# Interleaving the products of consecutive row pairs in the down projection

## The chip, the cores and the metric

The kernel runs on one core of a Trainium2 chip. The metric is device time in microseconds (us), the median of several executions. The engines are named as in the profile: PE (TensorE matmul), PEld (its weight loads), DVE (VectorE), ACT (ScalarE), POOL (GpSimd) and SP (SyncE, which here only issues DMAs).

## What is computed

One layer of a streaming encoder: adaptive RMSNorm, an input projection that feeds gated DeltaNet and windowed attention, an output projection, and a ConvFFN. The change lies in the last step, the down projection `y = mid @ w_down` with its gated residual:

```
h2 = rms_norm(x, norm2_w) * (1 + scale2) + shift2
u = h2 @ w_up
u_c = causal_dwconv(u_ext, ffn_conv_w) + ffn_conv_b
gt, up = jnp.split(u_c, 2, axis=-1)
x = x + gate2 * ((jax.nn.silu(gt) * up) @ w_down)
```

There are 640 tokens, 2048 model channels and 5632 hidden channels, all float32.

## The kernel before

A float32 product is made of three matmuls in a faster type: each operand is split into a high part (a cast on ACT) and a low part (source minus high part, on DVE), and high·high, high·low and low·high are summed in PSUM.

**The stage.** The down projection runs in `down` (lines 1984 to 2062). The first 4 of the 44 blocks of hidden channels are multiplied plainly. The other 40 form 5 groups of 8 blocks, and each group takes 8 **jobs**, one for each pair (f, f+8) of output row blocks. So there are 40 jobs (`njobs`, line 2027). A job is a 2x2 block product by Winograd's scheme in **seven products**, numbered 1 to 7. A product is 12 matmuls of 128 columns of weights against 320 tokens: 4 pieces of the contraction by 3 split parts.

**The order of a job.** `WINO` (line 18) gives 1, 5, 6, 2, 7, 3, 4. A job takes two PSUM tiles of two banks each (line 2038): `mmd` (called a) and `mm2` (called b; the profile calls it `mm`). Product 1 opens a bank of a, products 2 and 5 open the two banks of b. `ONTO` (line 19) lets the others accumulate on what is there: 6, 7 and 4 onto the bank of 1, 3 onto the bank of 5. After each product DVE adds what the bank then holds to an output tile `y` (line 2046), so a later product may write into the bank only after that addition has read it. The two tiles have two buffers each, so the next job starts on fresh ones.

**Weights.** SP loads a tile `raw` of weights; two serve a job. ACT casts it (`whi`), DVE subtracts (`wlo`); products 5, 6, 7 and 3 need a sum of two weight blocks first (`wsum`), which DVE makes for 5, 6 and 3 and POOL for 7 (`DPOOL`, line 36). `next_unit` (line 396) keeps this three products ahead of the matmuls: the cast and the subtraction for the unit three later stand ahead of a product's matmuls in the program, and the addition `y` stands behind them. Each engine's queue is worked in order.

**The fill.** While a group's jobs run, `fill` (line 1936) prepares the operands of the next group. It loads blocks `mq` of the hidden activations, forms sums `t`, and splits each into `dop` (two operands, hi and lo). Its steps are slipped in between matmuls as a planner's clock allows.

**Output.** `y` is kept in DRAM (`yd`) between groups: a job's two tiles are loaded (`load`, behind the fourth product of the job before) and stored at the end (`late`, issued by `tail`). In the last group there is no fill; instead a residual tile `xo` is loaded from `xd` behind product 5, `resid` adds the gated result into it (`xo` and `rst` on DVE, a small `xo` on POOL) once a quarter of the output is complete, and each quarter is stored to `out_yT`. All these DMAs stand in the one queue of SP, in program order.

Of the kernel before, what the change touches and what calls it, by code (L numbers as in the profile page):

```python
# [6 lines left out]
F32 = mybir.dt.float32  # L7
# [3 lines left out]
ALU = mybir.AluOpType  # L11
# [3 lines left out]
P = 128  # L15
GRP = 4
ORDER = (2, 4, 5, 1, 6, 7, 3)
WINO = (1, 5, 6, 2, 7, 3, 4)
ONTO = {6: 1, 7: 1, 4: 1, 3: 5}
NF = 8  # L20
NP = 5
# [14 lines left out]
DPOOL = {7: 1}  # L36
# [191 lines left out]
class Kern:  # L228
# [81 lines left out]
    def build_stream(self):  # L310
        d = self.d
        self.units, self.upos, self.spos, self.apos, self.rpos = [], 0, 0, 0, 0
        self.rorder, self.rleft, self.rtile, self.utile, self.ltile = [], {}, {}, {}, {}
        for g in range(4):
            for i in range(3):
                self.add_unit(0, (("e", i, g), d["win"][i, :, g // 2, (g % 2) * 512:(g % 2 + 1) * 512]))
        for i in range(3, 44):
            self.add_block(("in", i), d["win"][i])
        for f in range(KC):
            self.add_block(("o", f), d["wo"][f])  # L320
        for f in range(KC - NF, KC):
# [12 lines left out]
        for i in range(NFF):  # L334
            quarters("u", i, ORDER[4:] if i < NP else ORDER, i < NP)
        n = 0
        for split, m in DGRP:
            for u in range(0 if split else 4 * m):
                self.add_unit(u % 2, (("d", n + u // 2), d["wdn"][n + u // 2]))
            for f in range(8 if split else 0):  # L340
                a = [[(("d", n + 2 * f + j), d["wdn"][n + 2 * f + j], r) for r in range(2)] for j in range(2)]
                t = {k: (("s", n + 2 * f, k), None, 0) for k in (5, 6)}
                for p, src, op in ((1, (a[0][0],), None), (5, (a[1][0], a[1][1]), ALU.add),
                                   (6, (t[5], a[0][0]), ALU.subtract), (2, (a[0][1],), None),
                                   (7, (a[0][0], a[1][0]), ALU.subtract), (3, (a[0][1], t[6]), ALU.subtract),
                                   (4, (a[1][1],), None)):
                    self.add_unit(tuple(x[2] for x in src), *(x[:2] for x in src), op=op, pool=DPOOL.get(p),
                                  keep=t[p][0] if p in t else None)
            n += 2 * m

    def issue_raw(self):
        while self.rpos < len(self.rorder) and not self.rleft.get(self.rraw.peek(), 0):
# [1583 lines left out]
    def fill(self, dp, c0, key):  # L1936
# [24 lines left out]

        for d in range(2):
            b = {}
            for n, (r, s) in enumerate(((0, 0), (0, 1), (1, 1), (1, 0))):
                b[r, s] = ox.tile([P, 2, HALF], F32, tag=f"ex{4 + n}", name="mq")
                k = c0 + 4 * r + 2 * d
                nc.sync.dma_start(out=b[r, s], in_=self.mdt[k:k + 2, :, s * HALF:(s + 1) * HALF].rearrange(
                    "k p c -> p k c"))
            t1, t2, t3, t4 = (dp.tile([P, 2, HALF], F32, tag="stg", name=f"t{n + 1}", bufs=4) for n in range(4))
            yield from put(1, b[0, 0])  # L1970
            yield (b[0, 1],)
            v.tensor_tensor(out=t1, in0=b[0, 1], in1=b[0, 0], op=ALU.subtract)
            yield from put(5, t1)
            yield (b[1, 1],)
            v.tensor_tensor(out=t3, in0=b[1, 1], in1=b[0, 1], op=ALU.subtract)
            v.tensor_tensor(out=t2, in0=t3, in1=b[0, 0], op=ALU.add)
            yield from put(6, t2)
            yield from put(2, b[1, 0])
            yield from put(7, t3)
            yield from put(3, b[1, 1])  # L1980
            v.tensor_tensor(out=t4, in0=b[1, 0], in1=t2, op=ALU.subtract)
            yield from put(4, t4)

    def down(self, dp):
# [11 lines left out]
        def tail():  # L1996
            while late:
                late.pop(0)()
# [16 lines left out]
            return [self.yd[n % 8 + 8 * i].rearrange("p (s c) -> p s c", s=2) for i in range(2)]  # L2015

        def load(n):
            ts = [ox.tile([P, 2, HALF], F32, tag=f"ex{2 * (n % 2) + i}", name=f"y{i}") for i in range(2)]
            for t, d in zip(ts, rows(n)):
                nc.sync.dma_start(out=t, in_=d)  # L2020
            return ts
# [5 lines left out]
        njobs = 8 * (len(DGRP) - 1)  # L2027
        ys = {0: load(0)}
        dest = {1: (0, 0), 5: (1, 1), 6: (0, 1), 2: (0, 0), 7: (1, 1), 3: (0, 1), 4: (1, 0)}
        for n in range(njobs):  # L2030
            f, g = n % 8, n // 8
            last = g == len(DGRP) - 2
            if f == 0 and not last:
                lane.add(self.fill(dp, DGRP[0][1] + 8 * (g + 1), g + 2))
            while g + 1 not in self.dops:
                self.pump()
            self.ops = self.dops[g + 1]
            a, b = self.main_ps2(0)[0], self.main_ps2(1)[0]
            banks = {1: a[:, 0, 0:HALF], 2: b[:, 0, 0:HALF], 5: b[:, 1, 0:HALF]}
            for q, pr in enumerate(WINO):  # L2040
                ps = self.product(pr, None, 1, banks[ONTO.get(pr, pr)], pr not in ONTO)
                if f == 7:
                    self.done.add(("p", g + 1, pr))
                r, h = dest[pr]
                y = ys[n][r][:, h]
                v.tensor_tensor(out=y, in0=y, in1=ps, op=ALU.add)
                if q == 1:
                    tail()
                if q == 3 and n + 1 < njobs:
                    ys[n + 1] = load(n + 1)  # L2050
                if q == 1 and last:
                    x = [dp.tile([P, 2, HALF], F32, tag="stg", name="xo", bufs=4) for _ in range(2)]
                    for i in range(2):
                        nc.sync.dma_start(out=x[i], in_=self.xd[f + 8 * i].rearrange("p (s c) -> p s c", s=2))
                if last and q > 2:
                    k = f + 8 * r
                    self.resid(dp, "rst", x[r][:, h], y, 5, k, h)
                    late.append(lambda x=x[r][:, h], k=k, h=h: nc.sync.dma_start(
                        out=self.o["yT"][:, k, h * HALF:(h + 1) * HALF], in_=x))
            if not last:  # L2060
                late.append(lambda n=n, ts=ys.pop(n): store(n, ts))
        tail()

# [135 lines left out]
```

## Time and profile before

| | us |
|---|---|
| median of 3 runs (3095.6 to 3096.77) | 3095.79 |
| the profiled execution | 3097.97 |
| its span, first to last instruction | 3096.2 |
| plain blocks end, 40 jobs begin (from the span's start) | 2547.4 |
| last group begins | 2973.9 |
| last instruction of DVE ends, about | 3091.7 |

The times below are microseconds from the start of the span. The 40 jobs are the last 544 us of it. Job 0 begins at 2547.4, job 11 at 2693.3, job 15 at 2748.0, jobs 20 to 22 run from 2816.3 to 2853.3, and the last group is jobs 32 to 39. In the timeline a matmul's duration (0.31) is longer than the distance to the next one, since matmuls overlap; the bracket at the end of a row is the time for which the engine sat idle before it, and what released it.

### The profile page before, as it was taken

The numbers are of one execution on the slowest core, as the hardware profiler recorded it, in microseconds if no ns is written. First come the engines' busy times: TensorE is split into PE (matmuls) and PEld (weight loads), VectorE is DVE, ScalarE is ACT, GpSimd is POOL, SyncE is SP. The second block draws the span as 40 slices with busy tenths as digits, with TensorE's granted clock in tenths as the row PEclk, the third lists the DMA queues.
The fourth block names the chain that finished last, engine by engine and source line by source line (L and its number), as shares of the span: only waits on it lengthen the run. The fifth ranks groups of instructions, "written<-read, shape, count | busy, mean of one in ns | idle before, by whom it ended". The sixth has DMA issues, their size and how long they took to land.

```text
span 3096.2 us, 52887 instructions
## 1 busy us (share of the span) xinstructions
PE 2943.2 (95%) x19649; PEld 2765.0 (89%) x19649; DVE 2291.0 (74%) x4419; ACT 1225.0 (40%) x2255; POOL 843.9 (27%) x1283
## 2 busy tenths in 40 slices
PE   5999999999999999987899999999999999999998
PEld 2688889998989988976899999999999999999987
DVE  4333436778886523599798899999899969989887
ACT  2332334333433312453344444444444454444432
POOL 2110012323333321266433333333333311111012
PEclk8999999999999999998999999999999999999999
DMA  8755532222223588646533333333332366655654
GB/s 339 283 179 177 189 119 84 77 79 78 87 76 120 192 292 299 215 137 197 177 97 103 107 97 98 103 102 97 107 105 96 96 226 204 216 193 199 206 201 162
DMA packets 219234, 480.73 MB, mean 155 GB/s; under 512 B 52082, under 2 KB 87184, under 8 KB 218960
## 3 DMA queue, kind: packets, MB, share of 16 engines
q1 hardware_dynamic: 185056, 429.99, 41.6%
q0 software_dynamic: 11152, 36.11, 3.5%
q10 hardware_dynamic: 22768, 11.25, 1.4%
q8 instruction: 155, 2.54, 0.3%
q14 instruction: 103, 0.84, 0.1%
HBM read 407.92 MB, written 71.18 MB: 155 GB/s over the span
## 4 chain that ended last, share of the span: by engine, by line
PE 41%; DVE 6%; DMA 3%; issue 2%; SPq 1%; POOL 0%; ACT 0%; DVEq 0%; POOLq 0%; ACTq 0%
PE mmd L90 21%; PE mm L90 19%; DVE wlo L90 2%; DVE y L90 1%; DVE dop L90 1%; DMA xo<-xd 1%; DVE wsum L90 1%; SPq L90 1%; DMA fext<-pd 1%; DMA y<-yd 1%; DVE t L90 1%; DVE ftm L90 0%; DMA e<-pd 0%; DVE xo L90 0%; DMA yd<-y 0%
## 5 line engine op out<-in xcount | busy, mean ns | idle before, releaser
L90 DVE TENSOR_TENSOR wlo<-raw,whi 128x512 fp32r<-128x512 f32 x584 | 441.4, 761 | 306.6 <-ACT whi L90 278.5
L90 ACT CAST whi<-raw 128x512 fp32r<-128x512 f32 x584 | 358.2, 619 | 553.6 <-PE mm L90 333.5
L90 ACT CAST whi<-wsum 128x512 fp32r<-128x512 f32 x600 | 367.2, 619 | 403.8 <-PE mmd L90 141.8
L90 DVE TENSOR_TENSOR wlo<-wsum,whi 128x512 fp32r<-128x512 f32 x600 | 422.7, 705 | 19.9 <-ACT whi L90 14.1
L90 DVE TENSOR_TENSOR wsum<-raw 128x512 f32<-128x512 f32 x455 | 357.1, 785 | 79.5 <-DMA raw<-in_wup 75.3
L90 PE MATMUL mm<-mh,wlo 128*128 128x320 f32 x1280 | 374.2, 313 | 10.1 <-DVE wlo L90 10.0
L90 PE MATMUL mm<-mh,whi 128*128 128x320 f32 x1280 | 373.8, 312 | 9.3 <-DVE qsq L90 8.1
L90 PE MATMUL mm<-ml,whi 128*128 128x320 f32 x1280 | 372.9, 312 | 0.6 <-DVE ml L90 0.6
L90 PE MATMUL mm<-hh,wlo 128*128 128x320 f32 x1376 | 331.4, 322 | 5.5 <-DVE wlo L90 5.5
L90 PE MATMUL mm<-hh,whi 128*128 128x320 f32 x1376 | 328.6, 320 | 4.5 <-ACT hh L90 3.2
L90 PE MATMUL mm<-hl,whi 128*128 128x320 f32 x1376 | 327.6, 320 | 0.3 <-DVE hl L90 0.3
L90 PE MATMUL mmd<-dop,whi 128*128 128x320 f32 x1280 | 287.2, 312 | 31.2 <-DVE y L90 29.8
L90 PEld LDWEIGHTS mm<-mh,wlo 128*128 128x128 f32 x1280 | 235.2, 189 | 24.0 <-DVE wlo L90 12.2
L90 PEld LDWEIGHTS mm<-mh,whi 128*128 128x128 f32 x1280 | 235.4, 189 | 20.5 <-issue 7.1
L90 PEld LDWEIGHTS mm<-hh,whi 128*128 128x128 f32 x1376 | 230.7, 191 | 21.9 <-issue 13.7
L90 PEld LDWEIGHTS mm<-hh,wlo 128*128 128x128 f32 x1376 | 231.5, 191 | 19.4 <-issue 11.6
L90 PEld LDWEIGHTS mmd<-dop,whi 128*128 128x128 f32 x1280 | 213.8, 189 | 39.1 <-ACT whi L90 25.7
L90 PEld LDWEIGHTS mm<-hl,whi 128*128 128x128 f32 x1376 | 230.9, 191 | 19.4 <-issue 16.5
L90 PEld LDWEIGHTS mm<-ml,whi 128*128 128x128 f32 x1280 | 235.2, 189 | 7.8 <-issue 6.7
L90 PE MATMUL mmd<-mh,wlo 128*128 128x320 f32 x768 | 233.2, 310 | 6.5 <-DVE wlo L90 6.5
L90 PE MATMUL mmd<-mh,whi 128*128 128x320 f32 x768 | 233.0, 310 | 1.1 <-ACT qacc L90 1.1
L90 PE MATMUL mmd<-ml,whi 128*128 128x320 f32 x768 | 232.7, 310 | 0.5 <-DVE ml L90 0.4
(418 smaller groups left out, 6397.3 us busy)
## 6 DMA issues: line engine op xcount, KB each, us to landing
raw<-in_wup SPq DMA_DIRECT2D x206, 512.0 KB, 3.7
araw<-in_adaw SPq DMA_DIRECT2D x256, 256.0 KB, 5.2
raw<-in_wdn SPq DMA_DIRECT2D x88, 512.0 KB, 4.1
raw<-in_win SPq DMA_DIRECT2D x82, 512.0 KB, 3.6
araw<-in_adaw SPq DMA_DIRECT2D x64, 512.0 KB, 6.3
yd<-y SPq DMA_DIRECT2D x80, 320.0 KB, 4.9
y<-yd SPq DMA_DIRECT2D x80, 320.0 KB, 3.8
raw<-in_wo SPq DMA_DIRECT2D x48, 512.0 KB, 5.3
```

The source lines that it names most:

```text
L90: return f(*args, **kw)
```

## The change

The seven products keep their formulas and their banks. Their order changes, and products of two consecutive jobs are interleaved. `PLACE` gives each product a place on a common scale, on which a job begins every 7 places. From the third job on, seven products in a row are 2 of job n, 7 of job n-1, 1 of n, 5 of n, 4 of n-1, 6 of n, 3 of n. The operands are filled in the order 2, 1, 5, 6, 3 and 7, 4 likewise. The output tiles `y` get three buffers for two, and two of the four `mq` tiles move to another pool. The load of the next job's `y` moves behind product 6 (it stood behind product 2, the fourth), that of `xo` behind product 2, the first, and stores are issued behind products 2 and 5.

```
-WINO = (1, 5, 6, 2, 7, 3, 4)
+WINO = (2, 1, 5, 6, 3, 7, 4)
+PLACE = {2: 0, 1: 2, 5: 3, 6: 5, 3: 6, 7: 8, 4: 11}
...
+    def djobs(self):
+
+        todo = sorted((7 * n + PLACE[p], n, p) for n in range(8 * (len(DGRP) - 1)) for p in PLACE)
+        return [x[1:] for x in todo]
...
-            for n, (r, s) in enumerate(((0, 0), (0, 1), (1, 1), (1, 0))):
-                b[r, s] = ox.tile([P, 2, HALF], F32, tag=f"ex{4 + n}", name="mq")
+            for n, (r, s) in enumerate(((1, 0), (0, 0), (0, 1), (1, 1))):
+                b[r, s] = (ox if n < 2 else dp).tile([P, 2, HALF], F32, tag=f"ex{6 + n}", name="mq")
...
+            yield from put(2, b[1, 0])
             yield from put(1, b[0, 0])
...
+            yield (t3,)
             v.tensor_tensor(out=t2, in0=t3, in1=b[0, 0], op=ALU.add)
             yield from put(6, t2)
-            yield from put(2, b[1, 0])
+            yield from put(3, b[1, 1])
             yield from put(7, t3)
-            yield from put(3, b[1, 1])
...
-            ts = [ox.tile([P, 2, HALF], F32, tag=f"ex{2 * (n % 2) + i}", name=f"y{i}") for i in range(2)]
+            ts = [ox.tile([P, 2, HALF], F32, tag=f"ex{2 * (n % 3) + i}", name=f"y{i}") for i in range(2)]
...
-        for n in range(njobs):
+        part, x = {}, {}
+        for n, pr in self.djobs():
...
+            ps = self.product(pr, None, 1, part[n][ONTO.get(pr, pr)], pr not in ONTO)
...
+            if pr in (2, 5):
+                tail()
+            if pr == 6 and n + 1 < njobs:
+                ys[n + 1] = load(n + 1)
+            if pr == 2 and last:
+                x[n] = [dp.tile([P, 2, HALF], F32, tag="stg", name="xo", bufs=4) for _ in range(2)]
+                for i in range(2):
+                    nc.sync.dma_start(out=x[n][i], in_=self.xd[f + 8 * i].rearrange("p (s c) -> p s c", s=2))
```

What this does to the queues, at two places. First DVE in a job without fill. `y0` and `y1` are the two output tiles of a job; the number behind `mmd` or `mm2` tells the jobs apart. Before, the additions are of products 6, 2, 7, 3 and 4 of one job:

```order
L90 TENSOR_TENSOR y0_31091<-y0_31091,mmd_31150 128x320
L90 TENSOR_TENSOR wsum_31209<-raw_31019 128x512
L90 TENSOR_TENSOR wlo_31212<-raw_30872,whi_31211 128x512
L90 TENSOR_TENSOR y0_31091<-y0_31091,mm2_31151 128x320
L90 TENSOR_TENSOR wsum_31234<-wsum_31209,raw_30935 128x512
L90 TENSOR_TENSOR wlo_31237<-raw_30935,whi_31236 128x512
L90 TENSOR_TENSOR y1_31092<-y1_31092,mmd_31150 128x320
L90 TENSOR_TENSOR wlo_31254<-wsum_31209,whi_31253 128x512
L90 TENSOR_TENSOR y0_31091<-y0_31091,mm2_31151 128x320
L90 TENSOR_TENSOR wlo_31273<-wsum_31234,whi_31272 128x512
L90 TENSOR_TENSOR y1_31092<-y1_31092,mmd_31150 128x320
```

In the changed program they are 7 of job n-1, 1 and 5 of job n, 4 of job n-1, 6 and 3 of job n:

```order
L91 TENSOR_TENSOR y1_30948<-y1_30948,mmd_30969 128x320
L91 TENSOR_TENSOR wlo_31153<-wsum_31110,whi_31152 128x512
L91 TENSOR_TENSOR y0_31087<-y0_31087,mmd_31108 128x320
L91 TENSOR_TENSOR wlo_31174<-wsum_31131,whi_31173 128x512
L91 TENSOR_TENSOR y1_31088<-y1_31088,mm2_31109 128x320
L91 TENSOR_TENSOR wlo_31191<-raw_30998,whi_31190 128x512
L91 TENSOR_TENSOR y1_30948<-y1_30948,mmd_30969 128x320
L91 TENSOR_TENSOR wsum_31207<-raw_31032 128x512
L91 TENSOR_TENSOR wlo_31210<-wsum_31169,whi_31209 128x512
L91 TENSOR_TENSOR y0_31087<-y0_31087,mmd_31108 128x320
L91 TENSOR_TENSOR wlo_31231<-raw_30998,whi_31230 128x512
L91 TENSOR_TENSOR y0_31087<-y0_31087,mm2_31109 128x320
```

One tile of PSUM was read at every second addition; now `mmd_30969`, `mmd_31108` and `mm2_31109` are each read at every third. The operations are the same ones.

Second, SP in the last group. Before:

```order
L90 DMA raw<-in_wdn 128x1024
L90 DMA out_yT<-xo 128x320 x4
L90 DMA xo<-xd 128x640 x2
L90 DMA raw<-in_wdn 128x1024
L90 DMA y_33222<-yd 128x640
L90 DMA y_33223<-yd 128x640
```

In the changed program:

```order
L91 DMA y_33385<-yd 128x640
L91 DMA y_33386<-yd 128x640
L91 DMA out_yT<-xo 128x320 x2
L91 DMA xo<-xd 128x640 x2
L91 DMA raw<-in_wdn 128x1024 x2
L91 DMA out_yT<-xo 128x320 x2
```

The load of `xo` stood behind a load of weights and four stores of outputs; now it stands behind the loads of `y` and two stores (of product 4 of the job before last and of product 3 of the last), and the two loads of weights follow it.

## Rows read from the trace of the kernel before

**Rows 1.** The page: busy time, share of the span and instructions of PE.
```profile
PE 2943.2 (95%) x19649; PEld 2765.0 (89%) x19649; DVE 2291.0 (74%) x4419; ACT 1225.0 (40%) x2255; POOL 843.9 (27%) x1283
```

**Rows 2.** Busy time of each engine in stretches of the jobs; granted clock, DMA.
```profile
core 0: us, PE busy (x) PEld busy (x) DVE busy (x) ACT busy (x) POOL busy (x), PEclk, DMA share, GB/s
2547.40:2973.90 426.50, 403.03 (x2690) 395.75 (x2689) 379.26 (x652) 177.29 (x303) 44.32 (x32) 1.00 0.61 204
2816.30:2853.30 37.00, 37.00 (x255) 37.00 (x254) 30.54 (x52) 13.07 (x21) 3.91 (x3) 1.00 0.59 196
...
2706.00:2711.00 5.00, 3.09 (x14) 3.12 (x15) 3.42 (x7) 0.76 (x2) 0.00 (x0) 0.76 0.35 133
...
2973.90:3091.70 117.80, 102.05 (x676) 98.75 (x674) 97.79 (x197) 32.92 (x53) 29.16 (x38) 1.00 0.53 182
2986.80:3063.20 76.40, 63.93 (x422) 61.59 (x421) 62.57 (x126) 21.73 (x35) 20.14 (x25) 1.00 0.56 194
```

**Rows 3.** Waits of PE, jobs 0 to 31: us in total, times, longest.
```profile
PE mmd L90 <- DVE y L90: 15.3, 18, 2.0
PE mm L90 <- DVE y L90: 5.7, 6, 1.2
PE mmd L90 <- ACT whi L90: 1.2, 2, 0.7
```

**Rows 4.** Waits of PE in the last group.
```profile
PE mmd L90 <- DVE y L90: 14.5, 13, 1.7
```

**Rows 5.** Waits of DVE in the last group.
```profile
DVE xo L90 <- DMA xo<-xd: 10.8, 6, 2.3
```

**Rows 6.** Timeline in job 15: start, us, engine, operation, idle before it.
```profile
2752.16 0.48 DVE L90 TENSOR_TENSOR y<-y,mm 128x320 f32<-128x320 f32 x1
...
2757.48 0.81 DVE L90 TENSOR_TENSOR t<-mq,t 128x640 f32<-128x640 f32 x1
2758.21 0.48 DVE L90 TENSOR_TENSOR y<-y,mm 128x320 f32<-128x320 f32 x1
...
2758.84 0.53 PE L90 MATMUL mm<-dop,whi 128*128 128x320 f32 x2 [1.15 <-DVE y L90]
```

**Rows 7.** Timeline of DVE in job 20, without fill.
```profile
2823.47 0.68 DVE L90 TENSOR_TENSOR wlo<-raw,whi 128x512 fp32r<-128x512 f32 x1
2824.07 0.47 DVE L90 TENSOR_TENSOR y<-y,mm 128x320 f32<-128x320 f32 x1
2824.46 0.68 DVE L90 TENSOR_TENSOR wsum<-wsum,raw 128x512 f32<-128x512 f32 x1
```

**Rows 8.** Groups of DVE instructions in the jobs: busy, mean ns | idle before.
```profile
L90 DVE TENSOR_TENSOR wsum<-raw 128x512 f32<-128x512 f32 x39 | 41.2, 1055 | 0.0
L90 DVE TENSOR_TENSOR wsum<-raw,wsum 128x512 f32<-128x512 f32 x39 | 26.6, 683 | 0.0
```

**Rows 9.** Groups of POOL instructions in the jobs.
```profile
L90 POOL TENSOR_TENSOR wsum<-raw 128x512 f32<-128x512 f32 x39 | 53.4, 1369 | 401.3 <-DVE wlo L90 389.9 <-DVE dop L90 11.4
```

**Rows 10.** Chain of waits in job 35: start, us, what.
```profile
3021.77 0.33 SPq L90
...
3024.11 4.47 DMA xo<-xd
```

**Rows 11.** Timeline of DVE in job 35.
```profile
3026.04 0.49 DVE L90 TENSOR_TENSOR y<-y,mm 128x320 f32<-128x320 f32 x1
3028.70 0.48 DVE L90 SCALAR_TENSOR_TENSOR xo<-y,mod,xo 128x256 f32<-128x256 f32 x1 [2.17 <-DMA xo<-xd]
```

**Rows 12.** Timeline of SP ahead of job 11.
```profile
2689.05 1.98 SPq L90 DMA_DIRECT2D mq<-md  x4
2691.12 0.92 SPq L90 DMA_DIRECT2D y<-yd  x2
```

**Rows 13.** Timeline of DVE in job 11, the first addition.
```profile
2697.22 0.49 DVE L90 TENSOR_TENSOR y<-y,mmd 128x320 f32<-128x320 f32 x1 [1.81 <-PE mm L90]
```

**Rows 14.** Timeline of DVE in job 0, the first addition.
```profile
2552.23 0.49 DVE L90 TENSOR_TENSOR y<-y,mmd 128x320 f32<-128x320 f32 x1 [2.41 <-DMA y<-yd]
```

More of the change, by code (lines that the diff above doesn't have):

```diff
@@ L335, in build_stream @@
             quarters("u", i, ORDER[4:] if i < NP else ORDER, i < NP)
[L336 to L349, printed above, removed]
+        n = DGRP[0][1]
+        for u in range(16 * n // 4):
+            self.add_unit(u % 2, (("d", u // 2), d["wdn"][u // 2]))
+        for job, p in self.djobs():
+            f = 2 * n + 2 * job
+            a = [[(("d", f + j), d["wdn"][f + j], r) for r in range(2)] for j in range(2)]
+            t = {k: (("s", f, k), None, 0) for k in (5, 6)}
+            src, op = {1: ((a[0][0],), None), 5: ((a[1][0], a[1][1]), ALU.add), 6: ((t.get(5), a[0][0]), ALU.subtract),
+                       2: ((a[0][1],), None), 7: ((a[0][0], a[1][0]), ALU.subtract),
+                       3: ((a[0][1], t.get(6)), ALU.subtract), 4: ((a[1][1],), None)}[p]
+            self.add_unit(tuple(x[2] for x in src), *(x[:2] for x in src), op=op, pool=DPOOL.get(p),
+                          keep=t[p][0] if p in t else None)
+    def djobs(self):
+        todo = sorted((7 * n + PLACE[p], n, p) for n in range(8 * (len(DGRP) - 1)) for p in PLACE)
+        return [x[1:] for x in todo]
     def issue_raw(self):
@@ L2029, in down @@
         dest = {1: (0, 0), 5: (1, 1), 6: (0, 1), 2: (0, 0), 7: (1, 1), 3: (0, 1), 4: (1, 0)}
-        for n in range(njobs):
+        part, x = {}, {}
+        for n, pr in self.djobs():
             f, g = n % 8, n // 8
             last = g == len(DGRP) - 2
[L2033 to L2036, printed above, removed]
-            self.ops = self.dops[g + 1]
[L2038 to L2060, printed above, removed]
@@ new lines, in down @@
+            if pr == WINO[0]:
+                if f == 0 and not last:
+                    lane.add(self.fill(dp, DGRP[0][1] + 8 * (g + 1), g + 2))
+                while g + 1 not in self.dops:
+                    self.pump()
+                a, b = self.main_ps2(0)[0], self.main_ps2(1)[0]
+                part[n] = {1: a[:, 0, 0:HALF], 2: b[:, 0, 0:HALF], 5: b[:, 1, 0:HALF]}
+            self.ops = self.dops[g + 1]
+            ps = self.product(pr, None, 1, part[n][ONTO.get(pr, pr)], pr not in ONTO)
@@ new lines, in down @@
+            if f == 7:
+                self.done.add(("p", g + 1, pr))
+            r, h = dest[pr]
+            y = ys[n][r][:, h]
+            v.tensor_tensor(out=y, in0=y, in1=ps, op=ALU.add)
+            if last and pr in (1, 3, 7, 4):
+                k = f + 8 * r
+                self.resid(dp, "rst", x[n][r][:, h], y, 5, k, h)
+                late.append(lambda x=x[n][r][:, h], k=k, h=h: nc.sync.dma_start(
+                    out=self.o["yT"][:, k, h * HALF:(h + 1) * HALF], in_=x))
+            if pr in (2, 5):
+                tail()
@@ L2061, in down @@
+            if pr == 6 and n + 1 < njobs:
[4 more added lines that the diff above has]
+                    nc.sync.dma_start(out=x[n][i], in_=self.xd[f + 8 * i].rearrange("p (s c) -> p s c", s=2))
+            if pr == 4 and not last:
                 late.append(lambda n=n, ts=ys.pop(n): store(n, ts))
```

## The prediction

> **What bounds the kernel now.** The page first: PE is busy for 95% of the span [rows 1], so only where it is not can an order of products gain anything. Then the stretches of the jobs, since the change touches nothing before them. Jobs 20 to 22, which have no fill, take 37.00 us, 12.33 each, and PE is busy for all of it [rows 2]; that is the floor, 1.76 us for each of 280 products. Jobs 0 to 31 take 426.5 us, 31.9 over their floor of 394.6. The last group takes 117.8, 19.2 over its 98.6 [rows 2].
>
> Then what PE waits for there. In jobs 0 to 31 it waits 21.0 us in 24 waits for the addition `y`, and hardly for weights [rows 3]; in the last group 14.5 in 13, again for `y` [rows 4]. The sum, 35.5, is less than the excess of 51.1, because a wait costs more than its idle time: the start-to-start distance of matmuls is 1.76/12 = 0.147 us, and the overlap is lost at each restart. One wait of 2.0 us in job 11 was also followed by a fall of the granted clock to 0.76 over 2706 to 2711 [rows 2], that is a while at 1.2 GHz.
>
> Why is `y` late? DVE is in order, and in job 15 fill work (a `t`) stands ahead of `y` in its queue; `y` starts at 2758.21, PE resumes 0.15 us after its end, having waited 1.15 [rows 6]. That matmul opens product 3, the addition is of product 2, and the addition of product 5, whose bank product 3 uses, had been done since 2752.16. So the program waits by tile of two banks, not by bank. Before, then, products 6, 2, 7, 3 and 4 each wait for the addition two products earlier, and one product lies between.
>
> **The slack for DVE.** An addition lasts 0.48 and PE restarts 0.15 later; with some 0.1 before it starts, one product between gives 1.76 - 0.73 = 1.0 us by which DVE may be behind. Two products between give 2.8. The order of the additions shows that every tile is now read at each third one: 2, 5, 3 on b and 1, 6, 7, 4 on a.
>
> **What DVE has to do.** `wlo` and sums follow each other at 0.60, `y` at 0.39 [rows 7], so a job without fill is 10 x 0.60 + 7 x 0.39 = 8.7 us of DVE for 12.33 of PE. The sum that runs while POOL makes its own takes 1.055 in place of 0.683 [rows 8], 0.37 more in each job. A fill step of 640 columns takes 0.73 (2757.48 to 2758.21, [rows 6]); a group has 14 subtractions and 8 sums, 16 us over some five jobs. Jobs 0 to 31 thus fit on average (DVE busy for 379 us, PE's floor 395, [rows 2]), and only bunching hurts. In the new order I count at most 5 or 6 fill steps a job, 8.7 + 0.4 + 6 x 0.73 = 13.5, so 1.2 behind, and at most 3 in one product: two casts' subtractions and a sum, 2.3 us beside 1.6 of weights and `y`, 2.1 over 1.76. The worst place of a group therefore stands about 1.2 + 2.1 = 3.3 behind against a slack of 2.8.
>
> **Terms that stay, jobs 0 to 31.** Job 0: the first `y` waits for its load until 2552.23 [rows 14]. That load is not moved, but the first product that waits for an addition is now the fourth and not the third, so one product more covers it; I keep 1.0 us. Worst places: 0.5 us over, with a restart and what POOL adds, 1.2 in each of 4 groups, 5 us. From both sides: nothing (the slack holds), or half of the excess of today, 16 us (bunches meet). I take 5, since the count lies close to the slack. Stays 6; gains 31.9 - 6 = 25.9.
>
> **The last group.** Jobs 33 to 37 take 76.4/5 = 15.3 us, DVE busy for 12.5 of it [rows 2]. Here the bank is not the first cause: `xo` waits for its load, 10.8 us in 6 waits [rows 5]. In job 35 SP issues a load of weights at 3021.77, after the `wlo` that frees its buffer, then four stores, then `xo` at 3024.11, landed 4.47 later [rows 10]; DVE, idle for 2.17, uses it at 3028.70 [rows 11], and product 4 waits for what follows. In the new queue `xo` of job n+1 stands behind the store of product 3 of job n, and is first used after product 1 of job n+1. I follow this loop. From `xo` of product 1 to the end of `rst` of product 3 lie four products, 7.0 us, and the two residual operations, 0.6. POOL's part and its semaphores 0.7, one store issue 0.47 (four stores fill most of 3022.1 to 3024.1), and 4.6 from issue to use: 7.0 + 0.6 + 0.7 + 0.5 + 4.6 = 13.4 us per job. Without that loop DVE alone would need 12.5. So the group goes from 15.3 toward 13.4: 1.1 over the floor in 7 jobs is 7.7, of which 2 are taken up by the slack (2.8 less what fill left behind). Keep 5.7. Bounds: 0.2 x 7 = 1 if the load is early, and 17.6 (all of today's) if the loop is as slow as before.
>
> At the very end there is no job 40 to interleave with: 7 and 4 of job 39 stand side by side on a, and 4 waits for a whole addition, 0.1 + 0.48 + 0.15 + a restart, 0.85. What follows the last product (3090.1 to 3091.7, 1.6 us, and the last store) is the same. So 19.2 becomes 5.7 + 0.85 + 1.6 = 8.1; gain 11.1.
>
> **The other moves.** SP: the load of `y` stands two products later in the program, but SP runs ahead of PE; what holds it is the load of weights before it, freed by work of two products earlier, so it has some five products (8.8 us) before it is needed. It gets a third buffer for this, since the job before last is still open. With `mq` loads ahead of it, job 11 shows 6.1 us from its issue at 2691.12 to the addition at 2697.22, 1.81 of them DVE idle [rows 12, 13] (put down to PE, which had long been done). Covered: 0, and if not, the fourth rival. Weights: two jobs' tiles are held together in five buffers; by the order a buffer is freed nine products (16 us) before its next tile is needed, against a load of a few us. Numbers of operations on PE, DVE, ACT, POOL and SP are the same.
>
> **POOL and DVE.** A sum on POOL takes 1.37 us [rows 9], and it lengthens DVE's work by 0.37 [rows 8]; I used that. The Trainium skill, "SBUF — State Buffer", on its two physically separate sides, says that an operation of VectorE with two SBUF inputs and one of GpSimd lock a shared port pair for the whole instruction, so that one blocks the other fully. By that rule up to POOL's 1.37 are lost where the two meet, 1.0 more than the row shows; at the worst place of each of 4 groups that makes the sum 4 us higher.
>
> **Sum.** 25.9 + 11.1 = 37.0. The profiled execution took 3097.97, so 3061.0 like it; it lies 2.2 over the median, 3095.79, so the forecast is 3058.8.
>
> **Rivals.**
> - DVE becomes the bound. Bunches of fill meet and 16 us stay in jobs 0 to 31, and 13 of the last group: 51.1 - 29 - 2.5 = 20, 3076. For it: DVE is busy for 98 of 118 us in the last group. Against: its mean load leaves 16 us in jobs 0 to 31.
> - The loop through `xo` stays at 15.3 us, because SP meets another wait ahead of it (the store of product 3 waits for POOL): gain 25.9 + 1, 3069.
> - Everything hides, the load of `xo` too: only job 0, the last pair and the tail stay, 51.1 - 1.0 - 0.85 - 1.6 = 47.7, 3048.
> - The weights are next in line: where `y` is late, `wlo` ahead of it in the queue is late too, and PE waits there instead: 3096. Against: 1.2 us of such waits [rows 3], and weights are made three products ahead.
> - Slower: the load of `y`. If SP reaches it only at its place in the program, three products, 5.3 us, are left before the addition; each job that then pays as job 11 did loses 1.8 us on DVE with a restart and, in 32 jobs, some 60: 3095.8 + 60 - 37 = 3119. It decides from where `y` is issued less than 6 us before the first product of its job ends. Against: jobs 20 to 22 lose nothing today, [rows 2], and `y` gets more room than there.
> - It does not do what it says: if PE's wait went by something wider than the tile, each product would still wait for an addition close before it, and only the last group's 11 us would be gained: 3085. Against: PE went on while the operation behind that `y` was not yet needed, and product 5's bank mate alone explains the wait [rows 6].
>
> **Chances.** Forecast 0.48, DVE bound 0.17, `xo` loop 0.16, all hidden 0.10, weights 0.04, slower 0.03, not as it says 0.02. The range from 3048 to 3079 holds the first four with their unknowns. The forecast's own range is 3053 to 3066. A measurement of this kernel can tell about 0.2%, 6 us, from no change: faster 0.93 (all but weights and slower), same 0.04, slower 0.03.
>
> **What would show it.** Right: waits of PE for `y` in jobs 0 to 31 fall from 21 us to under 5, and none follows at products 2 and 3; jobs without fill keep 12.33; a job of the last group takes 13 to 13.6, with DVE still waiting for `xo` for about 1 us; DVE's busy time in the jobs is unchanged, its share of them rises. Wrong: PE waiting for `whi` or `wlo` by more than 5 us; `y` with DVE idle ahead of it at each job's first product; the last group still over 14.5 us per job.

## The result, and the profile of the changed kernel

| | before | changed |
|---|---|---|
| median, us | 3095.79 (5 runs, 3095.03 to 3097.82) | 3059.98 (5 runs, 3055.78 to 3065.51) |
| profiled execution / its span | 3097.97 / 3096.2 | 3059.98 / 3058.2 |
| jobs begin | 2547.4 | 2544.6 |
| jobs 0 to 31 (floor 394.6) | 426.5 | 405.6 |
| last group (floor 98.6) | 117.8 | 103.6 |

The ratio is 0.9883, with a 95% interval of 0.9869 to 0.9897: 36 us faster, against a forecast of 3058.8. The two traces differ by 38.0 us of span. Of these 35.1 lie in the 40 jobs, 20.9 in jobs 0 to 31 and 14.2 in the last group. Another 2.8 lie ahead of the jobs, where the programs are the same; over all the traces of this study that point lies between 2538.9 and 2550.0, whatever the kernel. So small differences are read below from the jobs' own stretch, and the median is quoted beside it.

The page of the changed kernel, its line of busy times, as [rows 1]:

```profile
PE 2930.0 (96%) x19649; PEld 2761.8 (90%) x19649; DVE 2292.9 (75%) x4419; ACT 1225.1 (40%) x2255; POOL 842.0 (28%) x1283
```

Busy times in stretches of it, with the columns of [rows 2]: jobs 0 to 31, the last group, four jobs of it, two jobs without fill:

```profile
2544.60:2950.20 405.60, 397.29 (x2690) 394.18 (x2688) 383.07 (x653) 176.50 (x303) 43.51 (x32) 1.00 0.63 214
2950.20:3053.80 103.60, 100.42 (x676) 98.76 (x674) 98.59 (x198) 32.55 (x53) 31.22 (x40) 1.00 0.63 207
2962.60:3011.80 49.20, 49.20 (x338) 49.20 (x336) 48.63 (x98) 17.31 (x28) 15.91 (x20) 1.00 0.74 244
2812.10:2836.70 24.60, 24.60 (x170) 24.60 (x169) 20.82 (x35) 9.34 (x15) 2.57 (x3) 1.00 0.57 193
```

The last two rows are the floor: 12.30 us per job as the stretches are cut, 12.32 from the first matmul of a job to that of the next. In the third DVE is busy for 48.63 of 49.20 us. What PE waits for in jobs 0 to 31 (two rows) and in the last group (one), and what DVE waits for from a DMA in the last group:

```profile
PE mm L91 <- DVE y L91: 4.8, 4, 1.5
PE mmd L91 <- DVE y L91: 3.4, 7, 0.8
...
PE mmd L91 <- DVE y L91: 1.6, 3, 0.7
...
DVE y L91 <- DMA y<-yd: 0.6, 2, 0.4
```

The 21.0 us of [rows 3] have become 8.2, the 14.5 of [rows 4] 1.6, and DVE's wait for `xo` [rows 5] is gone altogether.

### The profile page after: what moved, and what is told of

The parts are those of the page before. It is cut to its first block, busy times and chain, and to the rows that moved or that the text cites. A ratio compares the mean times of both kernels' runs of the same rounds, so it can differ in the third digit from the quotient of the medians.

```text
span 3058.2 us, 53007 instructions
## 1 busy us (share of the span) xinstructions
PE 2930.0 (96%) x19649; PEld 2761.8 (90%) x19649; DVE 2292.9 (75%) x4419; ACT 1225.1 (40%) x2255; POOL 842.0 (28%) x1283
## 4 chain that ended last, share of the span: by engine, by line
PE 75%; DVE 13%; DMA 5%; issue 4%; POOL 2%; ACT 1%; SPq 0%; DVEq 0%; ACTq 0%; POOLq 0%
PE mm L91 44%; PE mmd L91 20%; DVE wlo L91 4%; PE ada_ps L91 3%; DVE y L91 2%; PE inv_ps L91 2%; DVE wsum L91 1%; DVE dop L91 1%; DMA y<-yd 1%; DMA araw<-in_adaw 1%; PE pos L91 1%; DMA fext<-pd 1%; PE pstep L91 1%; PE pk L91 1%; DMA e<-pd 1%
## 5 line engine op out<-in xcount | busy, mean ns | idle before, releaser
L91 DVE TENSOR_TENSOR wsum<-raw 128x512 f32<-128x512 f32 x455 | 344.9, 758 | 79.2 <-DMA raw<-in_wup 75.2
L91 PEld LDWEIGHTS mm<-mh,wlo 128*128 128x128 f32 x1280 | 235.0, 189 | 23.9 <-DVE wlo L91 12.1
```

The costliest lines, as they stand in the source:

```text
L91: return f(*args, **kw)
```

## The experiments

They are told by question, not in the order of the runs; `...` in an edit marks lines left out. An excess is the time over the floors, 394.6 for jobs 0 to 31 and 98.6 for the last group.

### Does PE wait by tile or by bank? Product 2 on the tile of 1, 6, 7 and 4

```
-            banks = {1: a[:, 0, 0:HALF], 2: b[:, 0, 0:HALF], 5: b[:, 1, 0:HALF]}
+            banks = {1: a[:, 0, 0:HALF], 2: a[:, 1, 0:HALF], 5: b[:, 1, 0:HALF]}
```

> The kernel before with one thing changed: product 2 goes to the unused second bank of the tile of 1, 6, 7 and 4 (mmd), not to the bank beside that of product 5. The order is the old one, 1, 5, 6, 2, 7, 3, 4. No two products of a bank come closer by this. If PE waits by bank, product 2 still opens a bank of its own, product 7 still has one product between it and 6, and 3 now has none of its kind near: the kernel stays at 3095.8 or gains some us. If PE waits by tile, 2 must wait for the addition of 6 and 7 for that of 2, each with no product between: about 0.85 us twice in each of 40 jobs, 68 us, less what DVE gains from the slower pace and plus restarts: 3140 to 3175.

Measured: 3146.43 us, ratio 1.0163 (1.0149 to 1.0177). Jobs 0 to 31 take 476.5. The timeline of a job without fill, DVE's addition of product 6 and PE's first matmul of product 7 behind the addition of 2:

```profile
2848.37 0.49 DVE L90 TENSOR_TENSOR y<-y,mmd 128x320 f32<-128x320 f32 x1 [0.52 <-PE mmd L90]
2849.01 0.53 PE L90 MATMUL mmd<-dop,whi 128*128 128x320 f32 x2 [0.67 <-ACT whi L90]
2851.04 0.49 DVE L90 TENSOR_TENSOR y<-y,mmd 128x320 f32<-128x320 f32 x1 [0.63 <-PE mmd L90]
2851.67 0.53 PE L90 MATMUL mmd<-dop,whi 128*128 128x320 f32 x2 [0.67 <-DVE y L90]
```

Each addition ends 0.15 us before PE goes on (2848.37 + 0.49 to 2849.01, 2851.04 + 0.49 to 2851.67), and jobs that took 12.33 take 14.13. The first of the two waits is put down to `whi`, but PE starts 0.15 after `y` there too. Products 2, 6 and 7 use two banks, and 2 opens one that nobody reads; the program still waits. It is the tile, and a product right behind its tile mate costs 0.9 us ((14.13 - 12.33)/2).

### Is it the order that gained in jobs 0 to 31? The old order in the changed kernel

```
-WINO = (2, 1, 5, 6, 3, 7, 4)
-PLACE = {2: 0, 1: 2, 5: 3, 6: 5, 3: 6, 7: 8, 4: 11}
+WINO = (1, 5, 6, 2, 7, 3, 4)
+PLACE = {1: 0, 5: 1, 6: 2, 2: 3, 7: 4, 3: 5, 4: 6}
...
-            if pr in (2, 5):
+            if pr in (1, 2):
                 tail()
-            if pr == 6 and n + 1 < njobs:
+            if pr == 3 and n + 1 < njobs:
...
-            if pr == 2 and last:
+            if pr == 1 and last:
...
```

The fill's operands go back to their old order with it.

> The changed kernel with the old order of products, 1, 5, 6, 2, 7, 3, 4 without interleaving, also for the fill's operands; it keeps the rest of the change: three buffers of y, its load behind the sixth product of a job, xo loaded behind the first, stores issued behind the first and the fourth. If the spacing of the reads of a PSUM tile is what took the time in jobs 0 to 31, they go back from 405.6 to about 426 us, with PE again waiting some 20 us for y, at products 2, 7, 3 and 4. If the third buffer and the later load of y did it, they stay at about 406. The last group should stand where the old kernel with an early xo stands, since that is what is left in it: 109 to 111. Sum: about 3060 + 20.5 + 6.5 = 3087; by the rival 3066 or less.

Measured: 3090.07 us, ratio 0.9988 (0.9977 to 0.9998). The two stretches, and PE's waits in jobs 0 to 31:

```profile
2541.20:2967.10 425.90, 403.04 (x2690) 395.74 (x2689) 378.80 (x653) 177.20 (x303) 43.90 (x32) 1.00 0.61 204
2967.10:3083.90 116.80, 102.03 (x675) 98.73 (x674) 97.84 (x197) 32.91 (x53) 29.33 (x39) 1.00 0.56 184
...
PE mmd L91 <- DVE y L91: 14.1, 17, 2.2
PE mm L91 <- DVE y L91: 6.9, 7, 1.7
```

425.9 against 426.5 before: the order is all of the gain there. The third buffer and the later load of `y` give nothing by themselves; whether the new order needs them was not tried. On the last group the expectation was wrong, 116.8 for 109 to 111: in this kernel `xo` stands behind the store of product 4 again, which the old order finishes last, and DVE waits 9.7 us for it in 6 waits.

### What gained in the last group? Three kernels

First the kernel before, with `xo` alone moved ahead of the stores:

```
+                if q == 0 and last:
+                    x = [dp.tile([P, 2, HALF], F32, tag="stg", name="xo", bufs=4) for _ in range(2)]
...
                 if q == 1:
                     tail()
...
-                if q == 1 and last:
-                    x = [dp.tile([P, 2, HALF], F32, tag="stg", name="xo", bufs=4) for _ in range(2)]
...
```

> The kernel before, with one thing moved: in the last group xo is loaded behind product 1 and ahead of the four stores to out_yT, not behind product 5 and after them. The order of the products is the old one. Two theories of the last group's gain (117.8 us before, 103.6 after). By queue order alone the wait for xo was all of it: DVE's 10.8 us of waits for xo go, the group falls to about 104 to 106, and the kernel from 3095.8 to about 3083. By spacing alone the late xo was hidden behind waits that product 4, 3 and 7 have anyway with one product between: xo is no longer waited for, but PE still waits for y, the group keeps 113 to 118, and the kernel stays within 0.15% of 3095.8. I expect both in part: the group at about 109 to 111 and the kernel near 3088. Jobs 0 to 31 keep their 426 us by all of them.

Measured: 3084.39 us, ratio 0.9963 (0.995 to 0.9976). The last group, PE's wait in it and DVE's for `xo`:

```profile
2968.50:3076.40 107.90, 100.80 (x675) 98.66 (x673) 97.74 (x197) 32.94 (x53) 29.34 (x39) 1.00 0.59 199
...
PE mmd L90 <- DVE y L90: 5.7, 8, 1.0
...
DVE xo L90 <- DMA xo<-xd: 0.7, 1, 0.7
```

The group takes less than the 109 to 111 expected: 9.9 of the 14.2 us are the late load of `xo`, and can be had without the new order. What is left is one wait of 0.9 per job, of product 6 for the addition of 1, and that the new order takes away.

Then the changed kernel with `xo` late again:

```
-            if pr in (2, 5):
+            if pr in (2, 5) or last and pr == 7:
                 tail()
...
-            if pr == 2 and last:
-                x[n] = [dp.tile([P, 2, HALF], F32, tag="stg", name="xo", bufs=4) for _ in range(2)]
+            if last and (pr == 7 and n + 1 < njobs or pr == 2 and f == 0):
+                m = n + (pr == 7)
+                x[m] = [dp.tile([P, 2, HALF], F32, tag="stg", name="xo", bufs=4) for _ in range(2)]
...
```

> The changed kernel with the load of xo put back in the last group: xo of job n+1 is issued behind product 7 of job n and behind the store of that quarter. The order of the products is untouched. It tests the loop that the prediction followed (rst, POOL, store, load, xo). From xo of product 1 to the end of rst of product 7 lie six products, 10.6 us, then 0.6 + 0.7 + 0.9 for two issues + 3.8 us from issue to use as the changed kernel shows it: 16.6 us per job, or about 4 us of waiting on DVE per job that it can't make up, since it is 99% busy. Seven jobs at 4 us more: 3060 + 28 = 3088, the group at about 131. If the spacing absorbs a late xo (2.8 us of slack each time), the wait on DVE does not reach PE in full, and the group stays below 115, the kernel below 3072.

Measured: 3084.35 us, ratio 0.9963 (0.995 to 0.9976). The last group, PE's longest wait in it and DVE's for `xo` ("issue": a wait for nothing that the profile shows):

```profile
2950.10:3077.60 127.50, 107.60 (x675) 104.53 (x673) 97.39 (x198) 31.91 (x53) 31.06 (x40) 0.95 0.50 168
...
PE mm L91 <- DVE y L91: 15.5, 7, 2.7
...
DVE xo L91 <- DMA xo<-xd: 15.0, 4, 4.1
DVE xo L91 <- issue: 11.0, 3, 4.5
```

The group takes 23.9 us more, for 28 expected, with the granted clock at a mean of 0.95. Spacing does not absorb a late `xo`: in a quiet job DVE is busy for nearly all of the time (48.63 of 49.20 us above), so it can't make up what it waits. The loop of the prediction is real; the changed kernel just keeps out of it.

Third, whether the 0.9 of the old order is POOL's doing; `xo` early as above, and:

```
-DPOOL = {7: 1}
+DPOOL = {}
```

> The kernel before, old order of products, with two things together: xo of the last group loaded behind product 1 and ahead of the stores, and the sum for product 7 on DVE instead of POOL. It asks what of the last group's gain needs the new order at all. With xo early alone the group took 107.9 us, 13.3 per job, and product 6 waited 0.92 in each job for the addition of 1; POOL's sum, which runs at that place, holds DVE's xo operation for 1.29 us there. If that collision is the cause of the 0.92, the wait goes with POOL's sum: 12.32 to 12.5 per job, the group at 101.5 to 103, no worse than in the new order, which gave 101.3 without POOL. If one product of slack is too little for DVE at 99%, the waits stay: 13 or more per job, 106 to 110. Jobs 0 to 31 stay at 423 by both, as in the old order without POOL's sum alone, since xo isn't loaded there. Kernel: 3090.5 - 16 to 17 = 3074 by the first, 3079 to 3082 by the second. The distance to the best version of the new order, 3044.5, is then what the order itself is worth, 28 to 30 us, all of it in jobs 0 to 31.

Measured: 3080.93 us, ratio 0.995 (0.9936 to 0.9964). The last group:

```profile
2967.90:3075.20 107.30, 100.63 (x675) 98.66 (x673) 97.59 (x205) 32.94 (x53) 20.58 (x32) 1.00 0.60 200
...
PE mmd L90 <- DVE y L90: 3.2, 4, 0.9
PE mmd L90 <- ACT whi L90: 2.1, 3, 0.7
```

My first theory fell: 13.24 to 13.48 us per job from the second on, as with POOL's sum. All seven waits are at product 6, and in the three put down to `whi` too PE starts 0.15 us after the addition of 1 has ended. One product of slack is too little for DVE there, whoever makes the sum. In the new order without POOL's sum the group takes 101.3 (below), so spacing is worth 6.0 us of it, and 4.3 with POOL's sum (107.9 to 103.6).

### What stays in jobs 0 to 31? The fill, or POOL's sum beside DVE

The trace showed two suspects. In the timeline of the changed kernel in job 9, POOL's sum for product 7 begins just ahead of DVE's sum for product 3:

```profile
2658.95 1.30 POOL L91 TENSOR_TENSOR wsum<-raw 128x512 f32<-128x512 f32 x1 [12.16 <-DVE wlo L91]
2659.14 1.66 DVE L91 TENSOR_TENSOR wsum<-raw,wsum 128x512 f32<-128x512 f32 x1
```

and in the kernel before, in job 20:

```profile
2821.69 1.30 POOL L90 TENSOR_TENSOR wsum<-raw 128x512 f32<-128x512 f32 x1 [12.53 <-DVE wlo L90]
2822.07 0.49 DVE L90 TENSOR_TENSOR y<-y,mmd 128x320 f32<-128x320 f32 x1 [0.52 <-PE mmd L90]
2822.48 1.06 DVE L90 TENSOR_TENSOR wsum<-raw 128x512 f32<-128x512 f32 x1
```

In both, DVE's sum ends 0.55 us after POOL's (2660.80 after 2660.25, 2823.54 after 2822.99), and a DVE operation of 128x512, a sum or a `wlo`, does so behind 35 of the 39 sums of POOL that meet one in the changed kernel; in the other four the operation has another size and ends 0.28 to 0.68 after. The addition `y`, with one input in PSUM, keeps its 0.49. So a DVE operation with two SBUF inputs that begins while POOL works stands until POOL is done, and what it loses depends on where they meet: before, `y` lay under the first half of POOL's sum, and 0.37 were lost; now the sum itself meets nearly all of it, and 0.8 to 1.0 are. It also goes the other way, as here in the changed kernel:

```profile
2595.00 0.81 DVE L91 TENSOR_TENSOR dop<-mq,dop 128x640 fp32r<-128x640 f32 x1
2595.21 2.50 POOL L91 TENSOR_TENSOR wsum<-raw 128x512 f32<-128x512 f32 x1 [9.96 <-DVE wlo L91]
2595.74 0.81 DVE L91 TENSOR_TENSOR t<-mq 128x640 f32<-128x640 f32 x1
```

In all four cases where a `dop` is under way as POOL's sum begins, `dop` keeps its time and POOL takes 1.42 to 2.50 us for its 1.30; here the `t` behind it went ahead of POOL as well. The Trainium skill, "SBUF — State Buffer", on the two separate sides, has it that of an operation of VectorE with two SBUF inputs and one of GpSimd that reads SBUF, the one that starts first gets a shared port pair for its whole instruction, and the other blocks. These rows agree with it, and not with the mean of 0.37 that I went by.

First the changed kernel without the fill of groups 2 to 5:

```
-                if f == 0 and not last:
-                    lane.add(self.fill(dp, DGRP[0][1] + 8 * (g + 1), g + 2))
-                while g + 1 not in self.dops:
+                while 1 not in self.dops:
...
-            self.ops = self.dops[g + 1]
+            self.ops = self.dops[1]
```

> The changed kernel without the fill of groups 2 to 5: their operands aren't made, and the jobs of all groups read those of the first group (this part of the computation is left out). It tells what the fill costs in the new order, where the changed kernel has 11.0 us over the floor in jobs 0 to 31. If bunches of fill are the cause, as the prediction held, only the start of job 0 stays (1.75 us): jobs 0 to 31 take 396 to 397 us, 9 less, and the kernel 3051. If it is the collision of POOL's sum with DVE's alone, which needs no fill, waits of PE for y stay in many jobs: 401 or more, 3056.

Measured: 3049.86 us, ratio 0.9853 (0.9838 to 0.9868). Then without the sum for product 7:

```
-                       2: ((a[0][1],), None), 7: ((a[0][0], a[1][0]), ALU.subtract),
+                       2: ((a[0][1],), None), 7: ((a[1][0],), None),
```

> The changed kernel without the sum for product 7: that product takes a weight block as loaded in place of the difference of two (this sum is left out, on POOL and on DVE alike). DVE loses the 0.63 us per job that POOL's sum adds, and nothing else changes. If the collision makes up half of what stays in jobs 0 to 31, as the rule of the port would have it, the excess falls from 11.0 to about 6 us: 400.5, kernel 3054. If it has no part in it, the stretch keeps 404 to 406.

Measured: 3047.41 us, ratio 0.9849 (0.9835 to 0.9864). Jobs 0 to 31 of both, the one without fill first:

```profile
2539.20:2935.20 396.00, 394.44 (x2690) 394.21 (x2690) 332.88 (x545) 139.88 (x225) 41.20 (x32) 1.00 0.56 193
...
2543.40:2940.80 397.40, 394.54 (x2691) 394.27 (x2690) 361.02 (x654) 176.65 (x303) 0.00 (x0) 1.00 0.65 220
```

Either takes away nearly all. Without fill 1.4 us of excess stay, without the sum 2.8, and in both that is the start of job 0; jobs 1 to 31 keep 12.32 to 12.34. The question was put wrongly: it takes the fill and POOL's collision together to use up the slack.

Now the sum kept, but on DVE, in the changed kernel (the diff is the one line `DPOOL` again):

> The changed kernel with the sum for product 7 made on DVE, not on POOL. DVE gets 40 sums of 0.68 us more and loses what POOL's sum adds to its other sum (1.313 against 0.680 us in the changed kernel, 0.63 each), so its total work is the same within 2 us. If what stays over the floor in jobs 0 to 31 comes from single long collisions beside the fill (1.66 us instead of 0.68), they go and the 11.0 us fall to about 8; the last group keeps its 103.6 within 1 us; kernel about 3057. If collisions don't matter and only DVE's total load does, both stay within 1 us. If the sum for 7 stood better on POOL after all, because DVE has no room for it where the additions of 7 and 4 stand, the waits grow: 3063 or more.

Measured: 3051.34 us, ratio 0.9859 (0.9843 to 0.9876). The two stretches, and DVE's wait for `y` from the DMA in jobs 0 to 31:

```profile
2543.70:2945.30 401.60, 396.15 (x2690) 394.27 (x2689) 374.51 (x685) 177.00 (x303) 0.00 (x0) 1.00 0.66 216
2945.30:3046.60 101.30, 99.28 (x675) 98.66 (x673) 96.63 (x206) 32.94 (x53) 20.98 (x32) 1.00 0.65 211
...
DVE y L91 <- DMA y<-yd: 9.6, 5, 2.6
```

DVE makes 32 more sums in jobs 0 to 31 and is busy for 8.6 us less there (374.51 for 383.07): the sum on POOL cost DVE more than making it. The Trainium skill, "Perfetto Trace Analysis", on optimizing Scalar and DVE operations, says of work moved between these two that it might not help; here the sum on POOL is 6.3 us worse (405.6 + 103.6 us for the jobs, against 401.6 + 101.3). I had put DVE's total at the same within 2 us, by a mean that left out what the collision does to `wlo` and to the fill.

In the old order the same line does less:

> The kernel before with the sum for product 7 made on DVE, not on POOL; order and queues are the old ones. In the old order POOL's sum lengthened one of DVE's by 0.37 us (1.055 against 0.683), so DVE gets 0.31 us more of work per job. If total DVE work is what counts there, jobs 0 to 31 lose 1 to 4 us more than their 31.9, and the last group stays: 3097 to 3100. If single long collisions beside the fill made part of the old waits as well, it gains up to 5 us: 3091. By either the gain that the removal of POOL's sum brings in the new order, 8 us, would not be had in the old one.

Measured: 3090.55 us, ratio 0.9984 (0.9974 to 0.9993). Jobs 0 to 31 and the last group:

```profile
2541.90:2965.00 423.10, 402.20 (x2690) 395.80 (x2690) 381.36 (x683) 176.96 (x303) 0.00 (x0) 1.00 0.63 205
2965.00:3084.20 119.20, 103.34 (x675) 100.27 (x674) 97.80 (x205) 32.92 (x53) 20.52 (x32) 0.99 0.52 180
```

3.4 us better, 1.4 worse: DVE is busy for 2.1 us more in jobs 0 to 31 and yet waits cost less, as the second theory had it. The 3.4 are not a firm size. Two more kernels here repeat these jobs exactly (those with `xo` moved): with POOL's sum the stretch took 426.5 and 429.5 us, without it 423.1 and 424.2. By the interval the kernel as a whole is 0.07 to 0.26% faster, 2 to 8 us.

### A wait that DVE's lag had hidden, and the best version

Without POOL's sum, of jobs 0 to 31 only 0, 4, 11 and 27 lose anything (14.22, 14.18, 14.02 and 14.18). In job 11, SP's issues and DVE's first addition:

```profile
2675.92 1.97 SPq L91 DMA_DIRECT2D mq<-md  x4
2677.93 0.95 SPq L91 DMA_DIRECT2D y<-yd  x2
...
2684.62 0.49 DVE L91 TENSOR_TENSOR y<-y,mm 128x320 f32<-128x320 f32 x1 [2.56 <-DMA y<-yd]
```

That is the place of [rows 12, 13]: `y` behind the fill's loads, 6.7 us from issue to use. In the changed kernel DVE was too late to notice. So `y` is loaded behind product 5:

```
-            if pr == 6 and n + 1 < njobs:
+            if pr == 5 and n + 1 < njobs:
```

> The version without POOL's sum (its sum for product 7 is on DVE) and with one thing more: the load of the next job's y is issued behind product 5 and not behind product 6, so that it stands ahead of the fill's four mq loads in SP's queue, where it stood behind them. Without POOL's sum the jobs 4, 11 and 27 alone lose time, 1.86, 1.70 and 1.86 us, and in each DVE stands idle for about 2.5 us for y, loaded behind mq. If the place in the queue is the cause, these three go back to 12.32: jobs 0 to 31 from 401.6 to 396.3, the kernel from 3051.3 to 3046. If y is late because the transfers of mq share the DMA engines with it wherever it stands, the three jobs keep 1 us or more each: 399 and over.

Measured: 3053.49 us, ratio 0.9859 (0.9844 to 0.9873): the median is no better than the 3051.34 of the version ahead. In its trace the jobs begin at 2550.0, 6.3 us later than in the one it is compared with, which the edit has no part in. The jobs show the effect: jobs 11 and 27 take 12.32. Job 4 keeps 13.91; the planner puts `mq` ahead of `y` there still, and DVE waits 2.23 us. Then job 0's load too, made while the plain blocks run:

```
             tail()
+            if f == 10:
+                ys = {0: load(0)}
...
-            ts = [ox.tile([P, 2, HALF], F32, tag=f"ex{2 * (n % 3) + i}", name=f"y{i}") for i in range(2)]
+            ts = [ox.tile([P, 2, HALF], F32, tag=f"ex{2 * ((n + 2) % 3) + i}", name=f"y{i}") for i in range(2)]
...
-        ys = {0: load(0)}
...
```

> The version before with the load of job 0's y made during the plain blocks as well. Job 0 loses 1.83 us to that load without this. With POOL's sum the same edit had given 1.67 us in job 0 and lost 1.0 again in jobs 1 to 3, where DVE was behind. If POOL's collisions were what kept DVE behind there, nothing is lost again: jobs 0 to 31 take 394.6 to 395, the kernel 3044.5. If the fill alone does it, 0.5 to 1.0 comes back in jobs 1 to 3: 3045.5.

Measured: 3044.45 us, ratio 0.9831 (0.9817 to 0.9846), 15.5 us under the changed kernel. First the stretches of the version ahead (jobs 0 to 31), then of this one:

```profile
2550.00:2947.60 397.60, 394.65 (x2690) 394.18 (x2689) 374.80 (x685) 177.10 (x303) 0.00 (x0) 1.00 0.67 218
...
2543.90:2938.50 394.60, 394.60 (x2690) 394.27 (x2690) 374.54 (x685) 177.02 (x303) 0.00 (x0) 1.00 0.66 219
2938.50:3039.70 101.20, 99.20 (x675) 98.71 (x673) 96.58 (x206) 32.97 (x53) 20.99 (x32) 1.00 0.66 211
```

Jobs 0 to 31 are at their floor; here `mq` falls behind `y` in job 4 too. Of the 2.6 left in the last group 0.8 is the pair 7, 4 of job 39, and the rest what follows the last product.

The same start had been tried with POOL's sum, and with another order at the end:

```
+LASTP = {2: 0, 1: 0.5, 5: 2, 6: 3.5, 7: 5, 3: 6, 4: 7}
...
-        todo = sorted((7 * n + PLACE[p], n, p) for n in range(8 * (len(DGRP) - 1)) for p in PLACE)
+        m = 8 * (len(DGRP) - 1)
+        todo = sorted((7 * n + (LASTP if n == m - 1 else PLACE)[p], n, p) for n in range(m) for p in PLACE)
...
```

> The changed kernel with both ends of the stretch mended: the first job's y is loaded during the plain blocks (behind the eleventh, into the free third buffer), and the products of the last two jobs stand as 2, 1, 7', 5, 6, 4', 7, 3, 4, so that 3 lies between the last 7 and 4. Job 0 shows 1.68 us of PE waiting at product 5, whose tile product 2 shares, for an addition that waits 1.59 for y; that goes, 14.07 to 12.4. The end pair 7, 4 of job 39 waits 0.82 and 0.83; one of them goes. Sum: 3060 - 1.65 - 0.8 = 3057.5. Rival: DVE is 98% busy at the end, so that the closer spacing of 6, 7 and 4 there costs the 0.8 again or more: 3058.5 to 3060; and job 0 may wait for weights or for its own fill instead.

Measured: 3059.22 us, ratio 0.9882 (0.9867 to 0.9897), which can't be told from the changed kernel. Both stretches, and the timeline of the one long wait of PE that is new in the last group:

```profile
2543.40:2947.10 403.70, 397.62 (x2690) 394.26 (x2689) 383.81 (x653) 176.54 (x303) 42.80 (x32) 1.00 0.63 214
2947.10:3052.70 105.60, 101.72 (x675) 99.95 (x673) 98.57 (x198) 32.54 (x53) 30.78 (x40) 0.98 0.62 202
...
3039.81 0.48 DVE L92 SCALAR_TENSOR_TENSOR xo<-y,mod,xo 128x256 f32<-128x256 f32 x1 [1.78 <-DMA xo<-xd]
...
3041.68 0.47 DVE L92 TENSOR_TENSOR y<-y,mmd 128x320 f32<-128x320 f32 x1
...
3042.30 0.53 PE L92 MATMUL mmd<-dop,whi 128*128 128x320 f32 x2 [2.13 <-ACT whi L92]
```

Job 0 falls from 14.07 to 12.40, and jobs 1 to 3 lose again what DVE had been given in it (13.28 in job 1). At the end the group loses 2.0 us where 0.8 were to be gained. The wait is that of product 4 of job 38. It is put down to `whi`, but PE starts 0.15 us after the end of the addition of 7 of that job (3041.68 + 0.47 to 3042.30). That addition stands in DVE's queue behind the first use of job 39's `xo`, and DVE had stood 1.78 us for its load: product 1 comes one place earlier in this order, so the loop through `xo` has one product less and binds. Behind this wait the granted clock has a mean of 0.57 over 3043 to 3047, part of it at 1.2 GHz.

## The prediction against the runs, point by point

**What bounds the kernel.** Right. The wait goes by tile, the order alone took 20.3 us out of jobs 0 to 31 (425.9 to 405.6), none of PE's waits there was for `whi` or `wlo`, and quiet jobs kept 12.32. The rival that it doesn't do what it says is answered by the kernel with 2 on the other tile.

**Jobs 0 to 31: 6 us predicted to stay, 11.0 stayed.** The mechanism was right and the term too small, in both its parts. The start was put at 1.0, and job 0 shows 1.75: I counted the fourth product as the first that waits, but 5 lies on the tile of 2 and is the third. DVE's addition of 2, in job 0:

```profile
2549.38 0.49 DVE L91 TENSOR_TENSOR y<-y,mm 128x320 f32<-128x320 f32 x1 [1.59 <-DMA y<-yd]
```

The bunches were put at 5, by one place of 1.2 in each group, and made 9.3, by ten waits: product 4 waits seven times for the addition of 7, and product 5 three times for that of 2. The step that failed is "it lengthens DVE's work by 0.37 [rows 8]; I used that": 0.37 was a mean of [rows 8] for the old place in DVE's queue, not a price of the collision. With the whole sum of POOL lost, as the sentence beside it worked out, 10 would have stayed; that this is near to 11.0 is in part chance, since it still counts one place in each group. The runs without fill and without the sum show that both are needed; neither is the cause alone.

**The last group: 8.1 predicted, 5.0 stayed.** Here the term was too large. I had a job go round in 13.4 us through `xo`, DVE waiting 1 us each time. The loop of the changed kernel, timeline of jobs 35 and 36:

```profile
2998.55 0.22 DVE L91 TENSOR_TENSOR rst<-y,mod 128x64 f32<-128x64 f32 x1
...
2998.84 0.71 POOL L91 TENSOR_TENSOR xo<-xo,rst 128x64 f32<-128x64 f32 x1 [2.68 <-DVE rst L91]
...
2999.58 0.34 SPq L91 DMA_DIRECT2D out_yT<-xo  x1
2999.96 1.03 SPq L91 DMA_DIRECT2D xo<-xd  x2
...
3003.78 0.48 DVE L91 SCALAR_TENSOR_TENSOR xo<-y,mod,xo 128x256 f32<-128x256 f32 x1
```

From the end of `rst` to the issue of `xo` it takes 1.19 us, and I had 1.2. From issue to use I took 4.6, after the 4.47 of [rows 10], where four stores were on their way ahead of the load. With one store just ahead it was used 3.82 after its issue without a wait, and the loop closes in the 12.3 us of the floor. The kernel with `xo` late shows the loop bind: 14.9 to 18.0 us per job for the 16.6 worked out with the new landing time.

**The end.** 0.85 was right for 4 (0.83), but 7 cost 0.82 as well: with no product of a job 40 there, only 3 lies between it and 6, and DVE was behind. Of the rest of the 5.0, 1.2 us lie in jobs 37 and 38, where DVE falls behind, and most of what is left after the last product; without POOL's sum the 5.0 go to 2.7.

**The sum.** A gain of 37.0 was predicted from the jobs and 35.1 came in the two traces: 5.0 less than predicted in jobs 0 to 31, 3.1 more in the last group. In the medians it is 35.8, so the forecast was 1.2 off. It is better than its parts, by luck: two errors went opposite ways.

**The signs.** Two of those named for right held: no wait at products 2 and 3, and jobs without fill at 12.32. Three did not: PE's waits for `y` in jobs 0 to 31 fell to 8.2 and not under 5; a job of the last group takes 12.32 without a wait for `xo`, not 13 to 13.6 with one of about 1; and DVE's busy time in jobs 0 to 31 did not stay but rose by 3.8 us (379.26 to 383.07), for the collision costs more in the new order. None of the signs named for wrong came.

**Rivals.** DVE as the bound did not come. The loop of `xo` did not come in the changed kernel; it does with `xo` late, and at the end with product 1 one place earlier. That everything hides came true only with what the last version adds, but for the last group's 2.6 us. For the weights, the 1.2 us of [rows 3] that were held against that rival are 2.3 with the waits on `mm`, and no waits for weights: in all four PE starts 0.15 us after an addition has ended (in job 11 at 2697.85, the addition of [rows 13] at 2697.22 + 0.49). The load of `y`, the slower rival, cost PE nothing in the changed kernel beyond job 0 (DVE stood 0.6 us for it in one more job, and 0.6 in the last group). Its mechanism showed as soon as DVE was on time, at the price given, 1.7 to 1.9 us, but in three jobs and not in 32: `mq` is loaded only twice for each group, and stands just ahead of `y` in some of these places.

## What to carry to other kernels

Where PE accumulates again onto what another engine has to read first, count the products between two users of a tile, not of a bank, and interleave independent work until the reader's worst bunch fits. A collision between two engines has no mean price: find what stands in the other's queue at that place after the change, and take the whole instruction as the price where the traces show that one engine stands for the other. Don't take a wait by its label alone: where PE starts a fixed 0.15 us after an addition, it was the addition. After each gain look again at what the late engine had hidden; here a load that was too late all along became the next wait.

## What the runs showed of the hardware that was not expected

POOL's sum of 128x512 (1.30 us), once at work, stops a DVE operation with two SBUF inputs until it ends: DVE's sum of 128x512 then ends 0.55 us after POOL's, and lasts 1.66, 1.51 or 1.06 us, as it met POOL early or late, in place of 0.68. Where such a DVE operation is under way first, it keeps its time, and POOL takes up to 2.50. The addition `y`, with one input in PSUM, runs beside POOL at 0.49 against 0.47 to 0.49 elsewhere. That a sum taken off the busiest helper engine should make it busier, by 8.6 us in 32 jobs of the new order, was the surprise of the study; in the old order it made DVE less busy, by 2.1 (379.26 for 381.36).
